# A two-layer decoder step on one core: second-layer units reordered, convolution chains one by one, output tiles scaled from PSUM

## The chip, the cores and the metric

One core of a Trainium2 chip runs the whole kernel as one launch. The metric is the device time in microseconds of that launch. Engines are named as in the profile: PE (TensorE matmul), PEld (its weight load), DVE (VectorE), ACT (ScalarE), POOL (GpSimd), SP (SyncE, which here only issues transfers).

## The reference, cut to what matters

Two layers, 2048 prompt rows and 64 sample rows of width 1024, float32. Both layers share a frame: pre-norm, one input projection to six groups of 512 channels, two mixers, one output projection, post-norm, residual.

```python
h = rms_norm(x, pre_g);  z = einsum("btd,de->bte", h, w_in)       # 1024 -> 6*512
# layer 0: a 3-tap gated convolution and a pooling mixer
# layer 1:
u, v, gc, za, zb, gd = split(z, 6)
yc = u * (tril(W_s) @ layer_norm(v) + b) * silu(gc)               # rows mixed in chunks of 128
yd = silu(layer_norm(dwconv31(za * sigmoid(zb)))) * silu(gd)      # 31 taps over the rows
o = einsum("bte,ed->btd", concat([yc, yd]), w_out)                # 1024 -> 1024
x = x + rms_norm(o, post_g)
```

The convolution of layer 1 has 31 taps for each of 512 channels, and its layer norm needs all 512 channels of a row, so a row of yd exists only when the convolution of all four channel blocks has passed it.

## The kernel before

**Stages.** The work is a list of 82 units in six stages: stages 0 and 1 are the input projection of layer 0 for the first and second 1024 rows, stage 2 its output projection, stages 3, 4 and 5 the same for layer 1. The sample rows ride along in stages 1 and 4. A unit of an input projection makes two blocks of 128 channels for 1024 rows with seven products of 12 matmuls (84), each matmul 128x512. Every operand is split into a high and a low part (`Bh`/`Bl` for activations, `ahi`/`alo` for weights), and each product takes three matmuls. A unit of an output projection ("z tile", `unit_z`) makes 128 rows by 1024 columns with 48 matmuls, into two PSUM banks: one tile uses `bank_a` and `bank_c`, the next the two `bank_b`. There are 17 z tiles in each layer, the 9th to 17th of layer 1 being the second 1024 rows and the sample.

**Units of layer 1** (`UNITS_O`): `d` makes a block's convolution input (za, zb), `v` the rows to be mixed, `u` the gate and product of the mixed rows, `g` the gate of the convolution. The `u` units need the mixing that follows the second `v`.

**The convolution** runs on DVE. `Dc.c21` puts each finished block's `chain(...)` into the list `chains`; `conv_proc`, the process of lowest priority, gives out one DVE instruction at a time. A chain splits even and odd rows: 31 taps into two sums `fa` and `fc` in turn (L1431 to L1442), then 16 taps with summed weights `wsum` into `fc` alone (L1454, L1458). Before, up to two chains take turns. After each 1024 rows and four blocks, `ln_tile` (L1829) reads 128 rows back, transposes them (PE, `yt`), normalises, transposes again (`yb`), multiplies with the gate (DVE, L1867) and stores to `yd`, from which a z tile loads its weights-side operand `araw` (split by ACT into `ahi` and by DVE, L452, into `alo`).

**The end of a z tile** (`post`, L1934): ACT copies each PSUM bank to an SBUF tile `o` as soon as it is full (L1054), which frees the bank; then ACT squares both (`junk`, L1946, a sum in `ss`), POOL makes the reciprocal root `rr` (three small instructions, L713 to L715), DVE scales both halves by `rr` and `gpost` (L1952), adds the residual `xres` (L1955), and POOL issues the stores. In layer 0 the tile is then normalised again (L1972), transposed (`tp`) and stored as input of layer 1.

**What sets the order.** The order on every engine is written out when the program is built: `Plan` keeps estimated clocks of the engines, processes say when they may go on, and `take_bank`, `U.take` and `a_need` let the plan's clock run on until a bank, a slot or a weight is there. On the chip each engine runs its list in order and waits on semaphores.

```python
yield ("c", lambda: len(chains) > 0 and (chains[0][1] is not None or U.room(3 if pl.relax else 6)))
turn = (turn + 1) % min(2, len(chains))
```

## Time and profile before

| | |
|---|---|
| median of 3 runs | 1587.73 us (1587.39 to 1588.47) |
| the profiled execution | 1585.21 us |
| its span, first to last instruction | 1583.5 us |
| PE busy | 1477.1 us, 93% of the span, 6746 instructions |
| DVE, ACT, POOL busy | 1089.1 (69%), 799.1 (50%), 460.8 us (29%) |
| moved by DMA | 408.14 MB, mean 258 GB/s |

The page's chain of work that ended last is almost all PE. A busy share is a mean over six stages and says little; the rows further down are cut by stage. The stages begin, by the count of the projection's matmuls (line L902; 1008 for an input stage, 816 for an output stage), at 0, 314.7, 582.6, 797.7, 1069.6 and 1357.2 us, and the last matmul ends at 1569.95 us.

### The profile page before, as it was taken

Reading aid. Unit: us, or ns where it says so; the run is one execution under the profiler, and the core shown is the slowest. Engines: PE = TensorE matmul, PEld = TensorE weight load, DVE = VectorE, ACT = ScalarE, POOL = GpSimd, SP = SyncE. Lnnn points to the kernel's source line nnn. Section 1 sums busy time; section 2 is a strip of 40 time slices with the busy share of each in tenths; the row PEclk is TensorE's granted clock in tenths of the full one; section 3 lists DMA queues with packets and bytes.
Section 4 is the critical chain, followed back from the end, with each engine's and each line's share of the span. In section 5 each row is a group of like instructions: output and inputs, shape, how many; then the busy total and the mean of one; then the engine's idle time right before and its main releaser. Section 6 shows DMA issues by size and latency. Waiting matters only on the chain. (4 is left out here: it accounts for less than half of the span.)

```text
span 1583.5 us, 22268 instructions
## 1 busy us (share of the span) xinstructions
PE 1477.1 (93%) x6746; PEld 1195.2 (75%) x6746; DVE 1089.1 (69%) x1843; ACT 799.1 (50%) x1680; POOL 460.8 (29%) x865
## 2 busy tenths in 40 slices
PE   4499998899999999999989999989999999999796
PEld 3277887788888887877767888867888887788675
DVE  4866788775656566577667678877865869894431
ACT  5455344664555465466564655455454464525521
POOL 4134333121121205575741421010122022324321
PEclk9699999999999999999999999999999999999898
DMA  7356879888897888799999889897557678738541
GB/s 279 128 189 221 291 268 325 277 276 303 287 323 273 309 262 270 245 317 310 348 361 353 304 311 323 278 330 238 183 187 237 206 245 298 241 129 246 152 149 42
DMA packets 232347, 408.14 MB, mean 258 GB/s; under 512 B 28705, under 2 KB 78129, under 8 KB 232226
## 3 DMA queue, kind: packets, MB, share of 16 engines
q1 hardware_dynamic: 192194, 277.23, 53.9%
q0 software_dynamic: 40032, 129.48, 21.9%
q8 instruction: 53, 0.87, 0.2%
q14 instruction: 68, 0.56, 0.1%
HBM read 277.16 MB, written 129.45 MB: 257 GB/s over the span
## 5 line engine op out<-in xcount | busy, mean ns | idle before, releaser
L902 PE MATMUL bank_b<-Bh,alo 128*128 128x512 f32 (+1 forms) x848 | 341.3, 402 | 4.0 <-DVE alo L452 3.9
L902 PE MATMUL bank_b<-Bl,ahi 128*128 128x512 f32 (+1 forms) x848 | 335.9, 396 | 4.0 <-ACT ahi L285 4.0
L902 PE MATMUL bank_b<-Bh,ahi 128*128 128x512 f32 (+1 forms) x848 | 335.0, 395 | 0.0
L285 ACT CAST ahi<-araw 128x512 fp32r<-128x512 f32 (+1 forms) x404 | 239.5, 618 | 14.8 <-issue 3.8
L902 PE MATMUL bank_c<-Bh,alo 128*128 128x512 f32 (+1 forms) x496 | 200.4, 404 | 10.0 <-ACT Bh L285 7.1
L902 PE MATMUL bank_a<-Bh,alo 128*128 128x512 f32 (+1 forms) x496 | 201.0, 405 | 6.6 <-DVE alo L452 5.1
L902 PE MATMUL bank_c<-Bl,ahi 128*128 128x512 f32 (+1 forms) x496 | 198.0, 399 | 9.5 <-ACT ahi L285 6.2
L902 PE MATMUL bank_a<-Bl,ahi 128*128 128x512 f32 (+1 forms) x496 | 198.4, 400 | 8.2 <-ACT ahi L285 7.1
L902 PE MATMUL bank_a<-Bh,ahi 128*128 128x512 f32 (+1 forms) x496 | 197.1, 397 | 0.0
L902 PE MATMUL bank_c<-Bh,ahi 128*128 128x512 f32 (+1 forms) x496 | 197.0, 397 | 0.0
L902 PEld LDWEIGHTS bank_b<-Bh,alo 128*128 128x128 f32 (+1 forms) x848 | 159.3, 188 | 41.5 <-DVE alo L452 3.4
L902 PEld LDWEIGHTS bank_b<-Bl,ahi 128*128 128x128 f32 (+1 forms) x848 | 159.6, 188 | 40.2 <-ACT ahi L285 4.9
L902 PEld LDWEIGHTS bank_b<-Bh,ahi 128*128 128x128 f32 (+1 forms) x848 | 159.3, 188 | 38.8
L452 DVE TENSOR_TENSOR alo<-araw,ahi 128x512 fp32r<-128x512 f32 (+1 forms) x164 | 108.6, 681 | 70.5 <-ACT ahi L285 61.6
L902 PEld LDWEIGHTS bank_c<-Bl,ahi 128*128 128x128 f32 (+1 forms) x496 | 93.9, 189 | 31.9 <-ACT ahi L285 7.7
L902 PEld LDWEIGHTS bank_c<-Bh,alo 128*128 128x128 f32 (+1 forms) x496 | 94.0, 189 | 31.0 <-ACT Bh L285 7.5
L902 PEld LDWEIGHTS bank_a<-Bl,ahi 128*128 128x128 f32 (+1 forms) x496 | 94.1, 190 | 30.2 <-ACT ahi L285 9.1
L902 PEld LDWEIGHTS bank_a<-Bh,alo 128*128 128x128 f32 (+1 forms) x496 | 94.0, 189 | 27.3 <-DVE alo L452 5.5
L902 PEld LDWEIGHTS bank_a<-Bh,ahi 128*128 128x128 f32 (+1 forms) x496 | 94.0, 190 | 22.5
L902 PEld LDWEIGHTS bank_c<-Bh,ahi 128*128 128x128 f32 (+1 forms) x496 | 93.9, 189 | 22.3
L1454 DVE SCALAR_TENSOR_TENSOR fc<-fs,wsum,fc 128x512 f32<-128x512 f32 x120 | 89.9, 749 | 2.9
L674 DVE TENSOR_TENSOR Bl<-braw,Bh 128x512 fp32r<-128x512 f32 x116 | 73.4, 686 | 24.7 <-ACT Bh L285 24.4
(269 smaller groups left out, 2464.7 us busy)
## 6 DMA issues: line engine op xcount, KB each, us to landing
araw<-wx SPq DMA_DIRECT2D x144, 256.0 KB
araw<-wsd SPq DMA_DIRECT2D x144, 256.0 KB
alo<-wld SPq DMA_DIRECT2D x144, 256.0 KB
alo<-wlx SPq DMA_DIRECT2D x96, 256.0 KB
praw<-wi SPq DMA_DIRECT2D x72, 256.0 KB
araw<-yd SPq DMA_DIRECT2D x64, 256.0 KB
araw<-wi SPq DMA_DIRECT2D x48, 256.0 KB
wld<-alo POOLq DMA_DIRECT2D x48, 256.0 KB, 3.9
```

The source lines that it names most:

```text
L285: nc.scalar.copy(out=out, in_=in_)
L452: nc.vector.tensor_tensor(out=lo, in0=x, in1=hi.bitcast(F32), op=SUB)
L674: nc.vector.tensor_tensor(out=Bl[j][:, k, :], in0=r, in1=Bh[j][:, k, :].bitcast(F32), op=SUB)
L902: nc.tensor.matmul(out=out[:m], lhsT=w[k][:, :m], rhs=r[:, k, :], start=(start and k == 0 and w is l), stop=(stop and k == KH - 1 and w is ...
L1454: nc.vector.scalar_tensor_tensor(out=C, in0=sm[:, j:j + HM], scalar=w, in1=C, op0=MUL, op1=ADD if j else SUB)
```

## The change

Three things. In layer 1 the two `v` units come first, and each `u` unit stands behind a `d` unit. The chains run one by one, in the order they are made, and a chain may begin with 5 free slots rather than 6. In `unit_z` the copies out of PSUM are gone: ACT squares straight from the bank, POOL's `rr` follows at once, and DVE's scale reads the bank, which is free only then. `post` waits for four slots rather than two and takes its `o` tiles itself; in layer 1 its DVE steps go half by half (scale, add, store, scale, add, store), and near the end (when the last unit is current) SP issues the stores in place of POOL.

```diff
-UNITS_O = [_d(0), ("v", 0, 4, 5), ("v", 1, 6, 7), _d(1), _u(0), _u(1), _d(2), _u(2), _d(3), _u(3),
+UNITS_O = [("v", 0, 4, 5), ("v", 1, 6, 7), _d(0), _u(0), _d(1), _u(1), _d(2), _u(2), _d(3), _u(3),
...
@@ unit_z
-            o.append(U.take([P, 512], "o"))
-            at = act(out=o[n][:m], in_=bk[:m])
-            done_bank(key)
+            banks.append((bk, key))
+            junk = sp.tile([P, 512], mybir.dt.bfloat16, tag="junk", name="junk", bufs=1)
+            at = act(out=junk[:m], in_=bk[:m], func=AF.Square, accum_out=ss[:m, n:n + 1])
+        r = rsq(ss, m)
...
@@ conv_proc
+            yield ("c", lambda: len(chains) > 0 and U.room(3 if pl.relax else 5))
+            for cost in chains[0]:
+                yield ("d", cost)
+            chains.pop(0)
...
@@ post
-        yield ("c", lambda: U.room(2))
+        yield ("c", lambda: U.room(4))
...
+        def scale(h):
             yield ("d", st_cost(512))
-            nc.vector.scalar_tensor_tensor(out=o[h][:n], in0=o[h][:n], scalar=r[:n], in1=gpost[h][:n], op0=MUL, op1=MUL)
+            bk, key = banks[h]
+            nc.vector.scalar_tensor_tensor(out=o[h][:n], in0=bk[:n], scalar=r[:n], in1=gpost[h][:n], op0=MUL, op1=MUL)
+            done_bank(key)
...
+            if lay and st["cur"] + 1 == len(seq):
+                nc.sync.dma_start(out=dst, in_=o[h][:n])
+                U.free()
+            else:
+                store(dst, o[h][:n], *((U.free,) if lay else ()))
+        for f, h in ((scale, 0), (add, 0), (scale, 1), (add, 1)) if lay else ((scale, 0), (scale, 1), (add, 0), (add, 1)):
```

The order that the plan makes of it, at three places.

**Place 1: DVE, the end of the last convolution chain** (second 1024 rows, fourth block), in stage 5. L1458 is the chain's last step; the scale rows are z tiles. Before:

```order
L1454 SCALAR_TENSOR_TENSOR fc<-fs,wsum,fc 128x512 x5
L1952 SCALAR_TENSOR_TENSOR o<-o,rr,gpost 128x512 x2
L1955 TENSOR_TENSOR o<-o,xres 128x512 x2
L452 TENSOR_TENSOR alo<-araw,ahi 128x512
L1454 SCALAR_TENSOR_TENSOR fc<-fs,wsum,fc 128x512 x10
L1952 SCALAR_TENSOR_TENSOR o<-o,rr,gpost 128x512 x2
L1955 TENSOR_TENSOR o<-o,xres 128x512 x2
L1458 SCALAR_TENSOR_TENSOR glu<-fs,wsum,fc 128x256 x2
```

After (L1939 is the scale, L1944 the add):

```order
L1939 SCALAR_TENSOR_TENSOR o<-bank_b_104,rr,gpost 128x512
L1454 SCALAR_TENSOR_TENSOR fc<-fs,wsum,fc 128x512
L1944 TENSOR_TENSOR o<-o,xres 128x512
L1939 SCALAR_TENSOR_TENSOR o<-bank_b_105,rr,gpost 128x512
L1944 TENSOR_TENSOR o<-o,xres 128x512
L1454 SCALAR_TENSOR_TENSOR fc<-fs,wsum,fc 128x512 x2
L452 TENSOR_TENSOR alo<-araw,ahi 128x512
L1454 SCALAR_TENSOR_TENSOR fc<-fs,wsum,fc 128x512 x2
L1458 SCALAR_TENSOR_TENSOR glu<-fs,wsum,fc 128x256 x2
```

Before, the chain's end stands behind the scales of the fifth z tile of the stage; now behind those of the third. The fifth of the second half's nine gate products (L1867, now L1855), which the tenth z tile needs, stood behind the scales of the ninth tile and now stands behind those of the seventh.

**Place 2: DVE, from the last z tile of stage 2 into stage 3.** `bank_b_104` and `_105` hold the 16th tile, `bank_a` and `bank_c` the 17th; the first matmul of stage 3 writes `bank_a`. Before:

```order
L1952 SCALAR_TENSOR_TENSOR o<-o,rr,gpost 128x512
L1955 TENSOR_TENSOR o<-o,xres 128x512 x2
L674 TENSOR_TENSOR Bl_89<-braw,Bh_82 128x512 x3
L1930 TENSOR_TENSOR xres<-xres 128x512 x2
L1972 SCALAR_TENSOR_TENSOR xres<-o,rr,gpre_5443 128x512
L1972 SCALAR_TENSOR_TENSOR xres<-o,rr,gpre_5445 128x512
L1930 TENSOR_TENSOR xres<-xres 128x512 x2
L1952 SCALAR_TENSOR_TENSOR o<-o,rr,gpost 128x512 x2
```

After:

```order
L1939 SCALAR_TENSOR_TENSOR o<-bank_b_105,rr,gpost 128x512
L674 TENSOR_TENSOR Bl_86<-braw,Bh_79 128x512
L1944 TENSOR_TENSOR o<-o,xres 128x512
L674 TENSOR_TENSOR Bl_86<-braw,Bh_79 128x512
L1944 TENSOR_TENSOR o<-o,xres 128x512
L674 TENSOR_TENSOR Bl_86<-braw,Bh_79 128x512 x2
L645 TENSOR_TENSOR praw<-praw 128x512
L1939 SCALAR_TENSOR_TENSOR o<-bank_a,rr,gpost 128x512
L674 TENSOR_TENSOR Bl_89<-braw,Bh_82 128x512 x4
L1969 SCALAR_TENSOR_TENSOR xres<-o,rr,gpre_5443 128x512
L630 TENSOR_TENSOR plo<-praw,plo 128x512
L1969 SCALAR_TENSOR_TENSOR xres<-o,rr,gpre_5445 128x512
```

The 17th tile's first scale moved ahead of the second normalisation (L1969, was L1972) and of L1918 (was L1930), and the scale of `bank_c` follows the last row shown.

**Place 3: the last stores.** POOL's last rows before:

```order
L262 DMA o_xp<-o 128x512 x2
L713 TENSOR_TENSOR ss<-ss 128x1
L714 TENSOR_SCALAR ss<-ss 128x1
L715 TENSOR_TENSOR rr<-ss,half 128x1
L262 DMA o_xp<-o 128x512 x2
```

SP's last rows after, where before there were only the loads of `xres`:

```order
L1928 DMA xres<-x1d 64x512 x2
L1928 DMA xres<-x1d 128x512 x2
L1953 DMA o_xp<-o 128x512 x2
L1928 DMA xres<-x1d 128x512 x2
L1953 DMA o_xp<-o 128x512 x2
```

The stores of the last two z tiles moved from POOL to SP; POOL now ends with `rr`, and the last tile's `xres` loads stand behind the stores of the tile before it.

## Rows read from the trace of the kernel before

**Rows 1.** Stretch: length; busy (instructions) of PE, PEld, DVE, ACT, POOL; PEclk; DMA share; GB/s.

```profile
797.70:867.80 70.10, 60.41 (x251) 47.05 (x251) 50.49 (x85) 37.44 (x76) 23.42 (x34) 0.95 1.00 362
...
1084.00:1327.00 243.00, 242.83 (x1226) 202.49 (x1225) 180.45 (x319) 123.17 (x254) 42.35 (x74) 1.00 0.67 215
...
1380.46:1391.62 11.16, 11.16 (x49) 9.00 (x49) 9.96 (x16) 3.56 (x8) 3.31 (x5) 1.00 0.49 153
1449.45:1462.69 13.24, 12.75 (x61) 10.24 (x61) 6.14 (x12) 8.00 (x18) 7.02 (x13) 1.00 1.10 324
1462.69:1491.07 28.38, 19.30 (x83) 15.40 (x82) 14.16 (x24) 15.97 (x34) 10.85 (x21) 0.82 0.55 159
...
sum 1583.50, PE 1477.12 PEld 1195.17 DVE 1089.05 ACT 799.11 POOL 460.80; mean PE 123.09 PEld 99.60 DVE 90.75 ACT 66.59 POOL 38.40
```

**Rows 2.** PE in time: start, us, and in brackets idle before and what ended it.

```profile
1478.88 0.79 PE L902 MATMUL bank_a<-Bh,alo 128*128 128x512 f32 x1 [5.07 <-DVE alo L452]
```

**Rows 3.** DVE in time (start, us): last chain's begin and end, fifth gate product.

```profile
1341.82 0.70 DVE L1426 TENSOR_TENSOR fs<-glu 128x527 f32<-128x527 f32 x1
...
1421.64 0.88 DVE L1458 SCALAR_TENSOR_TENSOR glu<-fs,wsum,fc 128x256 f32<-128x256 f32 x2
...
1470.33 0.69 DVE L1867 TENSOR_TENSOR lny<-lny,lng 128x512 f32<-128x512 f32 x1 [0.40 <-ACT lny L287]
```

**Rows 4.** DVE in time: taps in turn, and ten taps into one sum.

```profile
1389.23 0.75 DVE L1442 SCALAR_TENSOR_TENSOR fc<-glu,cst,fc 128x512 f32<-128x512 f32 x1
1389.90 0.75 DVE L1433 SCALAR_TENSOR_TENSOR fa<-glu,cst,fa 128x513 f32<-128x513 f32 x1
...
1411.35 7.84 DVE L1454 SCALAR_TENSOR_TENSOR fc<-fs,wsum,fc 128x512 f32<-128x512 f32 x10
```

**Rows 5.** Groups by line and form: busy us, mean ns of one, idle before.

```profile
L285 ACT COPY o<-bank_b 128x512 f32<-128x512 f32 x32 | 18.7, 585 | 66.6 <-PE bank_b L902 64.7 <-issue 1.8
L287 ACT ACTIVATE ga<-bank_b 128x512 f32<-128x512 f32 x8 | 4.8, 595 | 7.6 <-PE bank_b L902 7.5
...
L1952 DVE SCALAR_TENSOR_TENSOR o<-o,rr,gpost 128x512 f32<-128x512 f32 x64 | 45.7, 753 | 34.6 <-POOL rr L715 34.6
L1131 DVE SCALAR_TENSOR_TENSOR win<-pm,cst,sgb 128x512 f32<-128x512 f32 x16 | 12.0, 750 | 14.3 <-PE pm L1127 13.4 <-PE pm L1125 1.0
```

**Rows 6.** In time: end of the tenth and 17th tile of stage 2, their scales.

```profile
710.41 0.57 ACT L285 COPY o<-bank_b 128x512 f32<-128x512 f32 x1
...
724.23 1.41 DVE L1952 SCALAR_TENSOR_TENSOR o<-o,rr,gpost 128x512 f32<-128x512 f32 x2
...
797.51 0.39 PE L902 MATMUL bank_c<-Bh,ahi 128*128 128x512 f32 x1
...
817.93 1.41 DVE L1952 SCALAR_TENSOR_TENSOR o<-o,rr,gpost 128x512 f32<-128x512 f32 x2
```

**Rows 7.** Waits of PE from 780 to 870.

```profile
PE bank_c L902 <- ACT ahi L285: 4.7, 3, 2.8
PE bank_c L902 <- ACT bank_b L285: 2.9, 1, 2.9
PE bank_a L902 <- ACT ahi L285: 2.1, 3, 1.0
```

**Rows 8.** Waits of PE from 582 to 798.

```profile
PE tp L1982 <- DVE xres L1972: 4.2, 3, 1.6
```

**Rows 9.** The end, in time: after the last matmul.

```profile
1571.22 0.63 ACT L287 ACTIVATE junk<-o 128x512 bf16<-128x512 f32 x1
...
1572.03 0.19 POOL L713 TENSOR_TENSOR ss<-ss 128x1 f32<-128x1 f32 x1 [6.48 <-ACT junk L287]
...
1573.18 1.42 DVE L1952 SCALAR_TENSOR_TENSOR o<-o,rr,gpost 128x512 f32<-128x512 f32 x2 [8.52 <-POOL rr L715]
...
1575.49 1.15 POOL L262 DMA_DIRECT2D o_xp<-o  x2 [2.35 <-DVE o L1955]
```

**Rows 10.** Transfers issued on POOL for the result: KB each, median us to landing.

```profile
o_xp<-o POOLq DMA_DIRECT2D x32, 256.0 KB, 3.0
```

More of the change, by code (lines that the diff above doesn't have):

```diff
@@ L1038, in unit_z @@
         m, t0 = (NSAMP, NPR) if i < 0 else (P, i * P)
-        o = []
+        banks, ss = [], sp.tile([P, 2], F32, tag="ss", name="ss", bufs=4)
         for n in range(2):
@@ L1052, in unit_z @@
                     a_done(u, h)
-            o.append(U.take([P, 512], "o"))
-            at = act(out=o[n][:m], in_=bk[:m])
-            done_bank(key)
+            banks.append((bk, key))
+            junk = sp.tile([P, 512], mybir.dt.bfloat16, tag="junk", name="junk", bufs=1)
+            at = act(out=junk[:m], in_=bk[:m], func=AF.Square, accum_out=ss[:m, n:n + 1])
+        r = rsq(ss, m)
         def go():
-            yield ("u", at)
-            yield from post(lay, t0, m, o, (i // 8 * 4 + i % 4, i % 8 // 4))
+            yield from post(lay, t0, m, banks, r, at + 2.2, (i // 8 * 4 + i % 4, i % 8 // 4))
         pl.spawn(go(), 2)
@@ L1485, in conv_proc @@
     def conv_proc():
-        turn = 0
         while True:
-            yield ("c", lambda: len(chains) > 0 and (chains[0][1] is not None or U.room(3 if pl.relax else 6)))
-            turn = (turn + 1) % min(2, len(chains))
-            if chains[turn][1] is None and not U.room(9):
-                turn = 0
-            c = chains[turn]
-            if c[1] is None:
-                if not U.room(3):
-                    continue
-                c[1] = next(c[0])
-                continue
-            yield ("d", c[1] + (0.12 if len(chains) == 1 else 0.0))
-            try:
-                c[1] = next(c[0])
-            except StopIteration:
-                chains.remove(c)
-                if st.get("conv_end") and not chains:
-                    return
+            yield ("c", lambda: len(chains) > 0 and U.room(3 if pl.relax else 5))
+            for cost in chains[0]:
+                yield ("d", cost)
+            chains.pop(0)
+            if st.get("conv_end") and not chains:
+                return
     class Dc:
@@ L1562, in proc @@
                     act(out=old[:, e, :], in_=g[e][:, HM:HM + HE], dep=pl.dve + 0.12)
-                chains.append([chain(self.s, self.cb, g[0], g[1]), None])
+                chains.append(chain(self.s, self.cb, g[0], g[1]))
             pl.spawn(proc(), 1)
@@ L1575, in smp @@
             aux_free()
-            chains.append([chain_s(cb, t), None])
+            chains.append(chain_s(cb, t))
     vs = {}
@@ L1932, in h_t, with post @@
                   lambda j=j: put(j, 0), U.free)
-    def post(lay, t0, n, o, ie=None):
-        xr = []
-        yield ("c", lambda: U.room(2))
+    def post(lay, t0, n, banks, r, at, ie=None):
+        xr, o = [], []
+        yield ("c", lambda: U.room(4))
         for h in range(2):
@@ L1942, in post, with add @@
             xr.append(t)
-        ss = sp.tile([P, 2], F32, tag="ss", name="ss", bufs=4)
-        junk = sp.tile([P, 512], mybir.dt.bfloat16, tag="junk", name="junk", bufs=1)
         for h in range(2):
-            at = act(out=junk[:n], in_=o[h][:n], func=AF.Square, accum_out=ss[:n, h:h + 1])
-        r = rsq(ss, n)
-        yield ("u", max(at + 2.2, xat))
+            o.append(U.take([P, 512], "o"))
         gpost, gpre = rows["gpost"], rows.get("gpre")
-        for h in range(2):
+        yield ("u", at)
+        def scale(h):
             yield ("d", st_cost(512))
-            nc.vector.scalar_tensor_tensor(out=o[h][:n], in0=o[h][:n], scalar=r[:n], in1=gpost[h][:n], op0=MUL, op1=MUL)
-        for h in range(2):
+            bk, key = banks[h]
+            nc.vector.scalar_tensor_tensor(out=o[h][:n], in0=bk[:n], scalar=r[:n], in1=gpost[h][:n], op0=MUL, op1=MUL)
+            done_bank(key)
+        def add(h):
             yield ("d", tt_cost(512))
@@ L1962, in post @@
                 dst = a["o_xp"][t0:t0 + n, c]
-            store(dst, o[h][:n], *((U.free,) if lay else ()))
+            if lay and st["cur"] + 1 == len(seq):
[4 more added lines that the diff above has]
+        for f, h in ((scale, 0), (add, 0), (scale, 1), (add, 1)) if lay else ((scale, 0), (scale, 1), (add, 0), (add, 1)):
+            if h == 0 and f is add:
+                yield ("u", xat)
+            yield from f(h)
         if lay == 1:
```

## The prediction, made blind

> **What bounds the kernel now.** I read the busy table by stretch first, then the waits of PE, then time lines of the places found. PE is busy 1477 of 1583.5 us [rows 1], so only some 106 us can be won without taking matmuls away, and the change takes none away. I therefore look for where PE stands still, and ask which of those places the change touches.
>
> The largest place behind the start is in stage 5. [...] The tile waits for its operand: its second half starts again at 1478.88, after 5.07 us of waiting for DVE's `alo` [rows 2]. That operand comes out of the fifth gate product of the second half, at 1470.33, and this out of the last convolution chain, which ends at 1422.5 (1421.64 + 0.88) [rows 3]. So the end of that chain sets 13 us of the program. The second place is the step from stage 2 to 3: 9.7 us idle of 70.1 (70.10 - 60.41) with the DMA engines at a share of 1.00 [rows 1]; 2.9 us of it waits for a PSUM bank and 6.8 for weight halves [rows 7]. The third is the end, 13.55 us after the last matmul at 1569.95.
>
> **The last chain ends earlier.** At place 1 of the order its last step moves from behind the fifth z tile's scales to behind the third's. The third tile is the undisturbed one, which ends at 1391.62 [rows 1]. Behind that come the square and `rr` (2.0 us, worked out at the end below), two scales and adds, five taps at 0.78 (7.84 for ten [rows 4]), a split and the last step; with what stands between, 10 us. The chain then ends near 1402, some 20 us earlier. From the chain's end to the fifth product 47.8 us passed (1470.33 - 1422.5), from there to the restart 8.6 (1478.88 - 1470.33) [rows 2, 3]: 1458, while the tile cannot begin before 1462.69 [rows 1]. The wait goes, with 4 us to spare; next late would be nothing that I can find in stage 5.
>
> What it is worth: the tenth tile holds 83 - 48 = 35 transposes, which must still be done. The ninth holds 13 in 13.24 us, 0.49 of them idle: (12.75 - 11.16) / 13 = 0.12 us each, so 4.3 us for 35. 28.38 - 11.16 - 4.3 = **12.9 us gained**. Bounds: nothing at all, and 12.9.
>
> **What the earlier end costs.** The first `d` unit comes two units later in each half, the second one later. That costs nothing while DVE has idle time to catch up: from 1084 to 1327 it is busy 180 of 243 us [rows 1]. One chain alone also makes each tap of its second part wait for the one before: 0.78 us apart instead of 0.67 for two sums in turn (1389.90 - 1389.23) [rows 4]. At most 15 taps in 8 chains, 13 us of DVE work, hidden by the same 63 idle us; 1.7 us in the last chain, inside the 4 to spare. The `u` units find their mixed rows as before, since one unit still lies between the second `v` and the first `u`.
>
> **No copies, scale from PSUM.** ACT loses 68 copies of 0.585 us [rows 5], 40 us, but it is busy half the time and this is on the path only at the end. A square read from a bank should cost what the gate read from a bank costs, 0.595 us, and DVE's scale reads a bank at the price of SBUF: 750 ns for the same form out of PSUM (L1131), 753 out of SBUF [rows 5].
> [...]
>
> The price is that a bank is held. Before, a copy freed it 0.6 us after its last matmul; now it waits for square, `rr` and DVE's turn. Inside a stage a bank is wanted again 11 to 12 us after its tile's end. In stage 5 DVE now does the scale 5 to 6 us after, so nothing waits. In stage 2 DVE is late at times: the tenth tile's scales ended 14.9 us (first of them, 724.98) after its last matmul near 710.1 [rows 6], which in the new kernel would be 2.7 us of waiting; but the scale now stands right behind the tile in DVE's order. I take 0, with bounds of -4.2 (the waits for `tp` gone [rows 8]) and +5 (two such tiles).
>
> At place 2 the wait is certain. Stage 3 begins with `bank_a`, and before its scale DVE has nine instructions of about 0.65 us in its order from the first scale of the 16th tile on: 9 x 0.65 + 0.75 = 6.6 us after the last matmul, if DVE comes to them on time; `rr` is ready by then. `bank_c` follows seven instructions later, at 11.9, and is wanted at 6.6 + 2.8 = 9.4: 2.5 more. Together 9.1. Against it stand the 9.7 us that PE idles there now; the loads go on during the new wait, so I let the waits for weight halves vanish in it: **0.6 gained**. Bounds: 5 gained, if DVE is ahead and only `rr` counts (2.0 + 0.75, then 2.5), and 14 lost, if the scale comes as late as it does today, 20 us after the last matmul (817.93 - 797.9 [rows 6]).
> [...]
>
> **The end.** Only the last half-tile's square is left behind the last matmul: from the square's start to POOL 0.81 us (1572.03 - 1571.22), POOL 1.15 (1573.18 - 1572.03) [rows 9]; so `rr` at 1569.95 + 2.0. Scale, add, scale, add take 2.9, and the last store is issued at 1574.85 rather than 1576.07: 1.2 us. Today 7.4 us pass from that issue to the end of the span, of which the landing takes 3.0 [rows 10]; the other 4.4 show no work. If they hang on POOL, which now ends with `rr`, up to 4.2 us go (1576.07 - 1571.9). I take **3.5**, near the upper bound because no row shows anything else to wait for; bounds 1.2 and 4.2.
>
> **Sum.** 12.9 + 0.6 + 3.5 = 17.0 us. The profiled execution took 1585.2 us, 2.5 under the median of the runs; against it 1568.2, against the median **1570.7 us**.
>
> **Rivals.**
> 1. *The normalisation, not the convolution, holds the tenth tile.* Its transposes now stand in PE's order between z matmuls, and POOL and ACT have to turn them round. For: only 4 us to spare. Against: the fifth product moved two tiles forward. Half of the 12.9 stays: 1577; all of it: 1583.6. Chance 0.10.
> 2. *Banks.* The scales come as late as today: 14 + 5 lost, 16.4 gained: 1590, no measurable change. For: DVE waits in order for transfers before them in stage 2. Against: the new order puts the scales ahead of those. Chance 0.08.
> 3. *The convolution does not catch up: slower.* Place: DVE in stage 4. If the 21.8 us by which the second `d` unit comes later (a unit with sample rows) carry through to the last chain's end, the tenth tile waits 21.8 longer instead of 12.9 less: +21.8 - 4.1, 1605. It decides from 7 us later than 1422.5 on. Against: DVE idles 63 us in that stretch. Chance 0.07.
> 4. *More goes.* The waits for weight halves and for `tp` vanish, the end gives 4.2: 12.9 + 5 + 4.2 + 4.2 = 26, 1561. Chance 0.13.
>
> **How the numbers follow.** The forecast has 0.62, alone 1564 to 1577. The range 1561 to 1584 takes in rivals 1 and 4 and leaves out 0.15. A measurement of this kernel can tell about 0.2% (3 us) from no change. Faster by more: forecast, rivals 1 and 4, 0.85. Within: rival 2, 0.08. Slower: rival 3, 0.07.
>
> **What would show it.** Right: the last L1458 in stage 5 near 1390 to 1405, the tenth z tile at 12 to 13 us with a granted clock of 1.00; 6 to 7 us of PE waiting for DVE before the first matmul of stage 3, and the loss of the stretch around it near today's 9.7; no wait of PE for a scale in stage 5; under 11 us from the last matmul to the end. Wrong: a wait for `alo` still standing in the tenth tile (rival 1), waits of PE for L1939 in stage 2 or over 12 us at stage 3 (rival 2), the last chain's end after 1425 (rival 3).

## The result, and the profile after

The changed kernel takes **1562.31 us** (median of 4 runs, 1559.45 to 1566.23) against 1587.56 us before in the same comparison (4 runs, 1586.87 to 1588.47): a ratio of **0.9842, 95% interval 0.9820 to 0.9864**, so 25.2 us faster where 17.0 were forecast. Its profiled execution took 1559.45 us with a span of 1557.7, 25.8 less than the span before. The measured time lies below the forecast's own band (1564 to 1577) and 1.3 us inside the range (1561 to 1584). One of the six executions of last_copied, a run further down, took 3432.05 us; what is said of that run goes by the other five.

The stages are cut in both traces at the first L902 matmul of each. Stages 0 and 1 took 557.1 us before and 556.6 after. The rest:

| | before | after | difference | forecast |
|---|---|---|---|---|
| stages 2 and 3 | 486.9 | 478.9 | -8.0 | -0.6 |
| stage 4 | 287.7 | 288.5 | +0.9 | 0 |
| stage 5 | 212.8 | 199.5 | -13.3 | -12.9 |
| last matmul to the end of the span | 13.6 | 8.3 | -5.3 | -3.5 |

Now the views. The busy table by stretch, columns as in [rows 1]: stage 3's first 70 us, and the ninth and tenth z tile of stage 5.

```profile
797.50:867.50 70.00, 68.99 (x315) 56.08 (x316) 30.36 (x55) 40.61 (x84) 25.11 (x48) 0.96 0.99 369
...
1445.48:1458.09 12.61, 12.61 (x63) 10.33 (x62) 7.54 (x13) 7.49 (x18) 6.24 (x12) 1.00 0.72 209
1458.09:1470.94 12.85, 12.63 (x62) 10.09 (x60) 8.26 (x14) 6.17 (x14) 6.29 (x13) 1.00 0.87 250
```

PE idles 1.0 us of the 70 where it idled 9.7, with the DMA engines as full as before (0.99, before 1.00). The stretch begins behind a wait of PE of 3.9 us, which is counted in stage 2. The tenth tile, whose wait for its operand the prediction starts from, takes 12.85 us at a granted clock of 1.00, before 28.38 at 0.82 [rows 1]. DVE in time: the last convolution chain's begin and end and the fifth gate product of the second half, which answer to [rows 3]:

```profile
1318.16 0.70 DVE L1426 TENSOR_TENSOR fs<-glu 128x527 f32<-128x527 f32 x1
...
1395.00 0.88 DVE L1458 SCALAR_TENSOR_TENSOR glu<-fs,wsum,fc 128x256 f32<-128x256 f32 x2
...
1443.36 0.69 DVE L1855 TENSOR_TENSOR lny<-lny,lng 128x512 f32<-128x512 f32 x1 [3.35 <-ACT lny L287]
```

The chain ends at 1395.9 (1395.00 + 0.88), before at 1422.5; the product comes 14.7 us ahead of the tenth tile (1458.09 - 1443.36), where it came 7.6 us after that tile had begun [rows 1, 3]. The waits of PE from 780 to 870, in place of [rows 7]:

```profile
PE bank_a L902 <- DVE o L1939: 3.9, 1, 3.9
PE bank_c L902 <- DVE o L1939: 1.0, 1, 1.0
```

In this stretch all waits for weight halves (`ahi`) are gone; two waits for scales have come. The groups by line and form, for [rows 5], show what the two operations that now read PSUM cost:

```profile
L1939 DVE SCALAR_TENSOR_TENSOR o<-bank_b,rr,gpost 128x512 f32<-128x512 f32 x32 | 23.3, 745 | 14.8 <-POOL rr L715 14.8
...
L287 ACT ACTIVATE junk<-bank_b 128x512 bf16<-128x512 f32 x32 | 19.1, 596 | 71.7 <-PE bank_b L902 61.8 <-issue 9.8
```

And the end in time, for [rows 9]; the last matmul ends at 1549.46:

```profile
1549.06 0.40 PE L902 MATMUL bank_b<-Bh,ahi 128*128 128x512 f32 x1
1549.55 0.60 ACT L287 ACTIVATE junk<-bank_b 128x512 bf16<-128x512 f32 x1 [4.92 <-issue]
...
1550.31 0.19 POOL L713 TENSOR_TENSOR ss<-ss 128x1 f32<-128x1 f32 x1 [10.08 <-ACT junk L287]
...
1551.45 0.75 DVE L1939 SCALAR_TENSOR_TENSOR o<-bank_b,rr,gpost 128x512 f32<-128x512 f32 x1 [8.31 <-POOL rr L715]
...
1552.95 1.73 SPq L1953 DMA_DIRECT2D o_xp<-o  x2
```

Both stores are issued by 1554.68; the span ends 3.0 us later. Before, 6.9 us passed between (1575.49 + 1.15 to 1583.5) [rows 9].

### The profile page after: what moved, and what is told of

It reads as the page before. It is cut to its first block, busy times and chain, and to the rows that moved or that the text cites. A ratio compares the mean times of both kernels' runs of the same rounds, so it can differ in the third digit from the quotient of the medians.

```text
span 1557.7 us, 22197 instructions
## 1 busy us (share of the span) xinstructions
PE 1471.7 (94%) x6746; PEld 1193.6 (77%) x6746; DVE 1090.8 (70%) x1843; ACT 769.3 (49%) x1616; POOL 446.3 (29%) x861
## 4 chain that ended last, share of the span: by engine, by line
PE 75%; issue 10%; DMA 5%; DVE 4%; POOL 3%; ACT 2%; SPq 0%; POOLq 0%; DVEq 0%; ACTq 0%
PE bank_b L902 31%; PE bank_c L902 18%; PE bank_a L902 18%; PE bank L902 1%; PE zs L913 1%; PE zs L914 1%; DVE Bl L674 1%; PE sg L1596 1%; PE tp L1979 1%; DMA sgd<-sgd 1%; DVE xT L796 1%; DMA wsd<-asum 1%; DVE xT L743 1%; PE zf L930 1%; ACT xrow L287 1%
## 5 line engine op out<-in xcount | busy, mean ns | idle before, releaser
L902 PE MATMUL bank_b<-Bh,alo 128*128 128x512 f32 (+1 forms) x848 | 340.2, 401 | 4.0 <-DVE alo L452 4.0
L902 PE MATMUL bank_b<-Bl,ahi 128*128 128x512 f32 (+1 forms) x848 | 335.7, 396 | 4.0 <-ACT ahi L285 4.0
L902 PE MATMUL bank_b<-Bh,ahi 128*128 128x512 f32 (+1 forms) x848 | 335.0, 395 | 0.0
L902 PE MATMUL bank_a<-Bh,alo 128*128 128x512 f32 (+1 forms) x496 | 202.2, 408 | 7.5 <-DVE o L1939 3.9
L902 PE MATMUL bank_c<-Bh,alo 128*128 128x512 f32 (+1 forms) x496 | 199.5, 402 | 8.0 <-ACT Bh L285 7.0
L902 PE MATMUL bank_a<-Bl,ahi 128*128 128x512 f32 (+1 forms) x496 | 198.2, 400 | 6.4 <-ACT ahi L285 5.3
L902 PE MATMUL bank_c<-Bl,ahi 128*128 128x512 f32 (+1 forms) x496 | 197.0, 397 | 5.1 <-DVE Bl L674 3.4
L902 PE MATMUL bank_a<-Bh,ahi 128*128 128x512 f32 (+1 forms) x496 | 197.2, 398 | 0.0
L902 PE MATMUL bank_c<-Bh,ahi 128*128 128x512 f32 (+1 forms) x496 | 196.2, 396 | 0.0
L902 PEld LDWEIGHTS bank_b<-Bh,alo 128*128 128x128 f32 (+1 forms) x848 | 159.1, 188 | 40.9 <-DVE alo L452 2.6
L902 PEld LDWEIGHTS bank_b<-Bl,ahi 128*128 128x128 f32 (+1 forms) x848 | 159.4, 188 | 40.4 <-ACT ahi L285 4.9
L902 PEld LDWEIGHTS bank_b<-Bh,ahi 128*128 128x128 f32 (+1 forms) x848 | 159.2, 188 | 38.5
L902 PEld LDWEIGHTS bank_c<-Bh,alo 128*128 128x128 f32 (+1 forms) x496 | 93.4, 188 | 29.5 <-ACT Bh L285 7.5
L902 PEld LDWEIGHTS bank_a<-Bh,alo 128*128 128x128 f32 (+1 forms) x496 | 94.0, 189 | 28.2 <-DVE o L1939 4.4
L902 PEld LDWEIGHTS bank_a<-Bl,ahi 128*128 128x128 f32 (+1 forms) x496 | 94.1, 190 | 27.2 <-ACT ahi L285 6.6
L902 PEld LDWEIGHTS bank_c<-Bl,ahi 128*128 128x128 f32 (+1 forms) x496 | 93.4, 188 | 27.4 <-DVE Bl L674 5.1
L902 PEld LDWEIGHTS bank_a<-Bh,ahi 128*128 128x128 f32 (+1 forms) x496 | 94.0, 190 | 22.7
L902 PEld LDWEIGHTS bank_c<-Bh,ahi 128*128 128x128 f32 (+1 forms) x496 | 93.4, 188 | 22.5
```

What stands on the lines that cost most here:

```text
L902: nc.tensor.matmul(out=out[:m], lhsT=w[k][:, :m], rhs=r[:, k, :], start=(start and k == 0 and w is l), stop=(stop and k == KH - 1 and w is ...
```

## The experiments

Three readings were to be separated: which part brings stage 5's 13 us, which brings the 8 us of stages 2 and 3, which the 5 us at the end. All twelve runs in one table; a time, where the edit starts from, and four lengths in us from each trace. "Chain end" is the end of the last L1458, counted from the first matmul of stage 5; "tile 10" goes from the tenth z tile's first matmul to the eleventh's (28.7 before by this cut).

| run | starts from | median | ratio to before, 95% interval | stages 2+3 | chain end | tile 10 | stage 5 | end |
|---|---|---|---|---|---|---|---|---|
| before | | 1587.6 | | 486.9 | +65.3 | 28.7 | 212.8 | 13.6 |
| after | | 1562.3 | 0.9842 (0.9820 to 0.9864) | 478.9 | +45.9 | 12.8 | 199.5 | 8.3 |
| f_order | before | 1602.0 | 1.0084 (1.0060 to 1.0108) | 489.8 | +88.2 | 27.6 | 229.5 | 12.9 |
| f_chain | before | 1570.3 | 0.9877 (0.9855 to 0.9899) | 486.8 | +9.1 | 11.2 | 198.0 | 13.3 |
| f_psum | before | 1576.4 | 0.9916 (0.9893 to 0.9940) | 480.9 | +66.1 | 26.7 | 209.8 | 11.5 |
| f_all_pool | after | 1566.8 | 0.9858 (0.9832 to 0.9884) | 476.5 | +45.9 | 13.0 | 199.6 | 11.3 |
| old_order | after | 1562.4 | 0.9849 (0.9823 to 0.9876) | 480.1 | -3.7 | 11.2 | 197.6 | 8.4 |
| b_room5 | before | 1574.4 | 0.9921 (0.9897 to 0.9945) | 484.3 | +14.6 | 11.1 | 200.4 | 13.6 |
| b_one6 | before | 1574.8 | 0.9916 (0.9895 to 0.9938) | 486.6 | +21.4 | 11.2 | 198.9 | 13.3 |
| room6 | after | 1593.5 | 1.0041 (1.0025 to 1.0058) | 478.7 | +89.9 | 27.3 | 230.1 | 8.6 |
| after_turns5 | after | 1565.9 | 0.9868 (0.9850 to 0.9886) | 479.9 | +61.9 | 19.3 | 207.5 | 8.3 |
| psum_copy | f_psum | 1592.4 | 1.0033 (1.0016 to 1.0050) | 491.2 | +69.6 | 27.0 | 213.1 | 9.8 |
| last_copied | after | 1568.5 | 0.9883 (0.9863 to 0.9903) | 483.2 | +45.7 | 12.8 | 201.1 | 8.0 |
| only_last | f_psum | 1591.2 | 1.0025 (1.0012 to 1.0038) | 490.7 | +66.1 | 26.8 | 211.3 | 12.7 |

Stage 0, which no edit touches, takes 288.7 to 293.1 us in these traces, and stages 2 and 3 of after and f_all_pool, where the programs are alike, differ by 2.4; a difference of 2 to 4 us in one trace proves little without its waits.

### Each part alone

**f_order**: the unit order alone.

```diff
-UNITS_O = [_d(0), ("v", 0, 4, 5), ("v", 1, 6, 7), _d(1), _u(0), _u(1), _d(2), _u(2), _d(3), _u(3),
+UNITS_O = [("v", 0, 4, 5), ("v", 1, 6, 7), _d(0), _u(0), _d(1), _u(1), _d(2), _u(2), _d(3), _u(3),
```

> Only the order of the second layer's units is changed (both v units first, each u behind a d); the chains still take turns and the output tiles are still copied out of PSUM. Theory (the 13 us of stage 5 come from the last chain's earlier end, which the one-by-one rule brings): in this kernel's order the last chain's end stands behind 12 scales of stage 5, before behind 10, after behind 6; so it ends about 11 us later than 1422.5, near 1433, the tenth z tile waits about as much longer (28 us becomes 35 to 40) and stage 5 grows by 7 to 12 us. Rival (the unit order frees DVE early and that gives the 13 us): the tenth tile shrinks to 13 us, stage 5 gives 13. On stage 3 the theory that the order brings its 7.8 us (v units load less work on DVE and ACT at the start) expects 264 us there instead of 272; the rival that the missing copies bring them expects 272. Sum: 1580 to 1597 by the theory, about 1567 by the rival.

Measured 1602.0 us, 14.5 over before and beyond the theory's range: the order alone makes the kernel slower. The chain ends 23 us later against the stage's start, more than the 11 expected, and stage 5 grows by 16.8. The place differs from what was expected: the tenth tile is not longer, the second (20.6 us) and the ninth (19.8) are. PE in time, in these three tiles:

```profile
1384.53 0.80 PE L902 MATMUL bank_a<-Bh,alo 128*128 128x512 f32 x1 [5.72 <-DVE alo L452]
...
1471.97 1.12 PE L1859 MATMUL yb<-ident,yv 128*128 128x128 f32 x4 [2.99 <-ACT yv L287]
...
1491.95 1.11 PE L1859 MATMUL yb<-ident,yv 128*128 128x128 f32 x4 [3.18 <-ACT yv L287]
...
1501.34 0.80 PE L902 MATMUL bank_a<-Bh,alo 128*128 128x512 f32 x1 [6.58 <-DVE alo L452]
```

The operands of z tiles are late in both halves. So the theory had the direction right, and the size and the tile wrong. Stage 3 gives nothing: 272.4 us, before 271.8. Its first four units take 100.1 us and the next six 120.3, where before they took 95.6 and 125.8; the mixing's matmuls have moved between them.

**f_chain**: the chains alone, one by one and begun with five free slots.

```diff
...
+            yield ("c", lambda: len(chains) > 0 and U.room(3 if pl.relax else 5))
+            for cost in chains[0]:
+                yield ("d", cost)
+            chains.pop(0)
...
```

> Only the chains are changed: one by one, begun with five free slots rather than six; unit order and copies out of PSUM as before. Theory: the last chain's end stands ahead of every scale of stage 5 (before behind 10), so it ends near 1365, the tenth z tile takes 12 to 13 us with the granted clock at 1.00, stage 5 falls from 212.8 to about 199.5: 1585 - 13 = 1572 to 1575. The rival by unit order expects the tenth tile unchanged, 1585 to 1588. Stage 3: 272 by both theories on it (neither the order nor the copies are touched), 264 only if the one-by-one chains are what relieves its start. End: 13.5 us from the last matmul, as before.

Measured 1570.3, 17.2 under before and 2 under the range; stage 5 at 198.0, nothing in stage 3 (273.4) or at the end. The tenth tile, columns as in [rows 1]:

```profile
1468.82:1479.98 11.16, 11.16 (x49) 9.00 (x48) 4.01 (x6) 3.56 (x8) 2.09 (x5) 1.00 0.48 152
```

It is as short as the undisturbed tile of [rows 1]. The chain part brings stage 5's gain by itself.

**f_psum**: squares and scales from PSUM, with all stores on POOL.

```diff
-            o.append(U.take([P, 512], "o"))
-            at = act(out=o[n][:m], in_=bk[:m])
-            done_bank(key)
+            banks.append((bk, key))
...
+            at = act(out=junk[:m], in_=bk[:m], func=AF.Square, accum_out=ss[:m, n:n + 1])
...
```

This part also moves the plan's wait for the residual's load (`xat`) from ahead of the scale to ahead of the add, which lets DVE's list have the scale earlier; no run takes that apart from the missing copies.

> Only the output tiles are changed: squared and scaled from PSUM, half by half in the second layer, with all stores still issued by POOL; unit order and chains as before. Theory: the last chain still stands behind 10 scales of stage 5, so the tenth tile stays at 28 us and stage 5 at 212.8. Stage 3: about 264 us if the missing copies and their slots are what let the weight halves come in time, 272 plus the wait for bank_a if not (272 to 277). End: 12.3 us from the last matmul (13.55 less 1.2) if the stores on SP make the rest, 8 to 9 us if the half-by-half steps make it all. Sum: 1577 to 1582.

Measured 1576.4, 11.1 under before. Stages 2 and 3 are 6.0 us shorter, the first four units of stage 3 alone 10.7 (95.6 to 84.9), the end 2.0 (between the two theories' numbers); the tenth tile stays at 26.7. PE in time at stage 3's start, its only waits there:

```profile
804.54 0.79 PE L902 MATMUL bank_a<-Bh,alo 128*128 128x512 f32 x1 [3.94 <-DVE o L1951]
...
810.62 0.50 PE L902 MATMUL bank_c<-Bh,alo 128*128 128x512 f32 x1 [0.60 <-DVE o L1951]
```

The gain in stages 2 and 3 comes with this part: 6.0 us alone, 8.0 in the changed kernel. By stage, f_chain's 14.7 (stage 5) and f_psum's 6.0 and 2.0, with 3.0 for SP below, make 25.7, about the whole difference of the two spans. That the sum comes so close is partly chance: in the changed kernel stage 5 gives 13.3, and the medians of the parts don't add up (17.2 and 11.1 under before, f_order 14.5 over).

**f_all_pool**: the changed kernel with its last stores on POOL.

```diff
-            if lay and st["cur"] + 1 == len(seq):
-                nc.sync.dma_start(out=dst, in_=o[h][:n])
-                U.free()
-            else:
-                store(dst, o[h][:n], *((U.free,) if lay else ()))
+            store(dst, o[h][:n], *((U.free,) if lay else ()))
```

> The changed kernel with the last stores issued by POOL again; all else as after. Theory (the stores on SP give some 4 of the 5.3 us at the end, since the program closes sooner behind a transfer of SP than behind one of POOL): 12 to 12.5 us from the last matmul to the end instead of 8.24, the time 3.5 to 4.5 us over the changed kernel's, near 1563.5 to 1566.5. Rival (squaring the last half alone and going half by half shorten the end): 8 to 9 us, no difference in time. Stages 2 to 5 as in the changed kernel by both.

The end takes 11.3 us, neither the 12 to 12.5 of the theory nor the rival's 8 to 9. So SP's stores bring 3.0 of the 5.3 (11.3 - 8.3), and the rest, 2.3, comes without SP. The medians differ by 4.5 us in the same sense, but the two intervals overlap. The last two issues in time; the span ends at 1561.7:

```profile
1554.14 0.61 POOL L262 DMA_DIRECT2D o_xp<-o  x1 [1.81 <-DVE o L1944]
...
1555.53 0.54 POOL L262 DMA_DIRECT2D o_xp<-o  x1 [0.78 <-DVE o L1944]
```

From the end of the last issue to the end of the span pass 5.6 us (1561.7 - 1556.07), with SP 3.0. What POOL does there is a closing DRAIN, an instruction at the end of its list that the view by source line shows; each row gives shortest, median and longest duration in ns, and first and last start. The long one is the first. Before, f_all_pool, after:

```profile
L2196 POOLq DRAIN  x3: 40/102/6366, 1576.1 to 1583.2; - x3
L2189 POOLq DRAIN  x3: 40/93/5384, 1555.5 to 1561.4; - x3
L2193 POOLq DRAIN  x3: 40/93/5096, 1550.8 to 1557.5; - x3
```

With the stores on POOL, the DRAIN begins at the last issue and ends about 1 us before the span does (1576.1 + 6.4 of 1583.5, 1555.5 + 5.4 of 1561.7). With the stores on SP it begins at POOL's last `rr` and is over 1.8 us before the end (1550.8 + 5.1 of 1557.7): it has run beside the last scales and stores. So SP's 3.0 us come from that overlap.

### Which condition lets the last chain end early

**old_order**: the changed kernel with the unit order of before.

```diff
-UNITS_O = [("v", 0, 4, 5), ("v", 1, 6, 7), _d(0), _u(0), _d(1), _u(1), _d(2), _u(2), _d(3), _u(3),
+UNITS_O = [_d(0), ("v", 0, 4, 5), ("v", 1, 6, 7), _d(1), _u(0), _u(1), _d(2), _u(2), _d(3), _u(3),
```

> The changed kernel with the unit order of before put back; one-by-one chains, scaling from PSUM and the last stores on SP stay. Theory (the order of the units gives nothing and costs 5 us early in stage 3, 24.9, 19.6, 23.9, 22.2 for its first four units where the kernel with scaling from PSUM alone took 24.6, 19.5, 19.5, 21.3; the other two parts give all): the last chain ends ahead of every scale of stage 5, stage 5 takes 198 to 199.5 us, stage 3 259 to 264, the end 8.3, and the time is 0 to 6 us under the changed kernel's 1562, near 1558. Rival (the parts need one another, the order keeps the chains' slots free once the output tiles hold them longer): stage 5 returns to 205 or more and the time to 1568 or more.

Measured 1562.4: the same time as the changed kernel, where some 4 us less was expected. The chain ends 50 us earlier against stage 5's start and that brings 1.9 us; it had been early enough. The 5 us that the order seemed to cost in stage 3's first units come back in the next six, as in f_order. So the new order neither brings nor costs anything that these runs can tell, once the other two parts are there.

**b_room5** and **b_one6**: the two conditions of the chain part, each alone, on the kernel before.

```diff
-yield ("c", lambda: len(chains) > 0 and (chains[0][1] is not None or U.room(3 if pl.relax else 6)))
+yield ("c", lambda: len(chains) > 0 and (chains[0][1] is not None or U.room(3 if pl.relax else 5)))
```

> The kernel before with one number changed: a chain may begin with five free slots rather than six; the chains still take turns. Theory (it is when the last chain may begin, not the turns, that set its end): it begins 168 projection matmuls ahead of stage 5 rather than 37 and ends behind 61 of them rather than 281, so the tenth z tile takes 11 to 13 us, stage 5 198 to 200 and the time is near 1572, as with the one-by-one chains. Rival (taking turns stretches each chain, and only one-by-one shortens it): the tenth tile keeps 20 us or more, 1580 or more.

```diff
-            yield ("c", lambda: len(chains) > 0 and U.room(3 if pl.relax else 5))
+            yield ("c", lambda: len(chains) > 0 and U.room(3 if pl.relax else 6))
```

This second diff starts from f_chain.

> The kernel before with the chains one by one, but a chain begins, as before, with six free slots. Theory (what counts is where the last chain's end stands in DVE's list, by whatever means it got there): it stands behind 92 projection matmuls of stage 5 and 2 scales (before 281 and 10), so the end comes near 1380, the tenth tile takes 11 to 13 us, stage 5 198 to 201, the time 1570 to 1576, as with either of the other two ways. Rival (the number five is needed, as in the changed kernel, where six cost 31 us of stage 5): the tenth tile keeps 20 us or more, 1580 or more.

Measured 1574.4 and 1574.8, tile 10 at 11.1 and 11.2 us, stage 5 at 200.4 (0.4 over its range) and 198.9: on the old order either condition is enough for the tenth tile. Both medians are 4 us over f_chain's, which the tenth tile does not explain.

**room6**: the changed kernel with six slots. The diff is that of b_one6.

> The changed kernel with one number put back: a chain begins with six free slots rather than five. Theory (the number is what lets the last chain begin): the chain begins behind 132 projection matmuls of stage 5 instead of 86 ahead of it, and ends behind 372 instead of 192, later than before (281); the tenth tile waits 27 us or more, stage 5 takes 213 to 235 us, and the time is 1575 to 1598. Rival (one-by-one alone gives the early end whatever the number): stage 5 at 199.5, 1562.

Measured 1593.5, slower than before; the chain ends 44 us later than in the changed kernel (+89.9 against +45.9) and stage 5 grows by 30.6. Here the ninth tile takes 32.5 us as well, by a wait of the same kind:

```profile
1465.47 0.80 PE L902 MATMUL bank_b<-Bh,alo 128*128 128x512 f32 x1 [6.76 <-DVE alo L452]
```

With the new order one-by-one needs the five.

**after_turns5**: the changed kernel with chains in turn, begun with five slots.

```diff
...
-            for cost in chains[0]:
-                yield ("d", cost)
-            chains.pop(0)
...
+            turn = (turn + 1) % min(2, len(chains))
...
+            yield ("d", c[1] + (0.12 if len(chains) == 1 else 0.0))
...
```

> The changed kernel with the chains taking turns again, two at a time, but begun with five free slots as in the changed kernel. In DVE's list the last chain's end then stands behind 254 projection matmuls of stage 5 and 8 scales (changed kernel 192 and 6, before 281 and 10). Theory (the place of that end in the list decides, and the tenth tile begins to wait once the end comes some 4 us later than 8 us behind the changed kernel's 1396): the end comes near 1407 to 1410, the tenth tile takes 13 to 20 us, stage 5 200 to 208, the time 1562 to 1571. Rival (five slots alone give all, as they did on the kernel before): the tenth tile at 12.8, stage 5 at 199.5, the time 1559 to 1565. Other rival (one-by-one is needed with the new order): the tenth tile at 25 or more, stage 5 at 212 or more, 1574 or more.

Measured 1565.9, chain end at 1410.3, tile 10 at 19.3, stage 5 at 207.5: the chain's end at the upper edge of the theory's numbers, the rest within them. Tile and stage lie outside both rivals' numbers; the time, 0.9 over the first rival's, does not tell the two apart. The tenth tile, and what PE waits for in it:

```profile
1457.66:1476.97 19.31, 15.26 (x70) 12.12 (x68) 11.20 (x19) 9.93 (x23) 8.82 (x15) 0.91 0.81 222
```

```profile
1464.97 0.66 PE L1859 MATMUL yb<-ident,yv 128*128 128x128 f32 x4 [3.48 <-ACT yv L287]
...
1466.20 0.80 PE L902 MATMUL bank_a<-Bh,alo 128*128 128x512 f32 x1 [0.58 <-DVE alo L452]
```

The waits make 4.1 us. Behind them the first matmul takes 0.80 us and the next six 0.63 each, where those at the tile's start take 0.39; the granted clock over the tile is 0.91. Read down the table, chain end against tile 10: up to +21.4 the tile takes 11.1 or 11.2 us, at +45.7 to +45.9 12.8 to 13.0, at +61.9 19.3, at +65.3 and later 26.7 to 28.7. Which edit brought the chain there makes no difference to the tenth tile. The step lies between +46 and +62. Where the chain ends later still (f_order, room6), the tenth tile grows no further; the ninth does (19.8 and 32.5 us).

### Where the waits for weight halves went

**psum_copy**: f_psum with a copy of each bank into the scratch tile `junk` ahead of the square; nothing reads it.

```diff
+            act(out=junk[:m], in_=bk[:m])
             at = act(out=junk[:m], in_=bk[:m], func=AF.Square, accum_out=ss[:m, n:n + 1])
```

> Scaling from PSUM alone, as in the earlier run, plus a copy of each bank into the scratch tile junk, read by nobody, ahead of each square: ACT's 68 copies of 0.585 us are back, but no slot is taken by them. Theory (what held the weight halves at stage 3's start was that a copy waited for a free slot, with the casts of the weights behind it on ACT): the first four units of stage 3 stay at 85 us and stage 3 at 262 to 264, since ACT waits for no slot; the time is within 3 us of 1576. Rival (ACT's time and place in its list): the four units return to 90 to 95 us, stage 3 to 270 or more, the time to 1583 or more.

Measured 1592.4, 16 over f_psum: the theory's time fails. Time and the first four units (92.7 us) are the rival's numbers, stage 3 (268.1) lies between the two. But the waits are not those of before. PE from 780 to 900:

```profile
PE bank_c L902 <- DVE o L1952: 4.6, 1, 4.6
PE bank_a L902 <- DVE o L1952: 4.0, 1, 4.0
PE bank_c L902 <- ACT ahi L285: 1.0, 1, 1.0
```

Weight halves stay nearly punctual although ACT has its copies back. That does not clear ACT's time, since PE waits 8.6 us for banks ahead of them, in which ACT can catch up. Stages 2 and 3 are 5 us longer each than in f_psum; 4.1 of these are longer waits for banks (8.6 against 4.5 us). The rest of the 16 was not traced.

**last_copied**: the changed kernel, with ACT's copy back for the last tile of stage 2 alone.

```diff
+        copied = lay == 0 and u + 1 == phase_units[ph][1]
...
+            if copied:
+                t = U.take([P, 512], "o")
+                act(out=t[:m], in_=bk[:m])
+                done_bank(key)
+                bk, key = t, None
             banks.append((bk, key))
...
```

> The changed kernel, but the last output tile of stage 2, and it alone, is copied out of PSUM again by ACT before it is squared and scaled. It asks where the weight halves' waits of stage 3 went (9.7 us of PE idle in its first four units before, 1.0 after, with 3.9 us of waiting for bank_a ahead of them). Theory (head start: PE's new wait for bank_a is what lets the weight halves get ahead, ACT casting them while PE stands): bank_a is free 0.6 us after its last matmul, the 3.9 and 1.0 us go, and the waits for ahi come back, 4 to 8 us in the first four units: no gain, 1560 to 1566. Rival (the missing copies and their slots relieve ACT's list, and the wait for bank_a is pure loss): neither wait is there, stages 2 and 3 together lose 4 to 5 us, the time is near 1557 and the best of all.

Measured 1568.5, 6.2 over the changed kernel and 2.5 beyond the head start's range; stages 2 and 3 make 4.3 of it. The waits for the banks are gone and those for weight halves are back: PE idles 8.0 us of the first four units (after: 1.0), 7.0 of it for `ahi`. PE in time:

```profile
804.80 0.80 PE L902 MATMUL bank_c<-Bl,ahi 128*128 128x512 f32 x1 [3.81 <-ACT ahi L285]
811.06 0.50 PE L902 MATMUL bank_b<-Bl,ahi 128*128 128x512 f32 x1 [0.77 <-ACT ahi L285]
819.25 0.50 PE L902 MATMUL bank_b<-Bl,ahi 128*128 128x512 f32 x1 [1.48 <-ACT ahi L285]
832.51 0.50 PE L902 MATMUL bank_c<-Bl,ahi 128*128 128x512 f32 x1 [0.97 <-ACT ahi L285]
```

**only_last**: the opposite. f_psum with copies for all tiles but the last of stage 2.

```diff
+        copied = not (lay == 0 and u + 1 == phase_units[ph][1])
...
```

> The kernel with scaling from PSUM alone, but only the last output tile of stage 2 is scaled from PSUM; all other output tiles are copied out first (and squared right behind the copy). Theory (head start): with PE waiting for bank_a before stage 3 as there, 2 to 8 us, the waits for ahi in the first four units fall from 9.7 us before to 0 to 3. Rival (it is the copies of all the tiles, in ACT's list and in the slots, that make the weight halves late): the waits for ahi stay at 6 to 10 us and the wait for bank_a stands on top of them. Stage 5 and its tenth tile as before by both (212 us; the last chain stands behind 10 scales), the time 1578 to 1595.

Measured 1591.2. PE waits once, for 14.1 us rather than 2 to 8, and in the four units behind that it idles 0.6 us; they take 84.0 us. PE, and below it DVE, in time:

```profile
814.41 0.80 PE L902 MATMUL bank_a<-Bh,alo 128*128 128x512 f32 x1 [14.09 <-DVE o L1957]
```

```profile
810.95 1.42 DVE L1936 TENSOR_TENSOR xres<-xres 128x512 f32<-128x512 f32 x2 [4.50 <-DMA td<-xres]
812.29 1.41 DVE L1984 SCALAR_TENSOR_TENSOR xres<-o,rr,gpre 128x512 f32<-128x512 f32 x2
813.61 0.74 DVE L1957 SCALAR_TENSOR_TENSOR o<-bank_a,rr,gpost 128x512 f32<-128x512 f32 x1
```

By the waits for `ahi` the head start holds in both directions. In all fourteen traces: wherever PE waits for `bank_a` ahead of stage 3 (after, f_psum, f_all_pool, old_order, room6, after_turns5, psum_copy, only_last), the waits for weight halves in the first four units come to 1.0 us or nothing. Wherever it doesn't (before, f_order, f_chain, b_room5, b_one6, last_copied), PE idles 8 to 10 us there, spread over the units.

The traces also show who gets ahead. Before, ACT is busy for 8.28 of the 8.31 us between the last matmul of stage 2 (it ends at 797.90 [rows 6]) and the cast of `ahi` that PE waits for. ACT, then PE:

```profile
806.21 1.12 ACT L285 CAST ahi<-araw 128x512 fp32r<-128x512 f32 x2
```

```profile
806.86 0.80 PE L902 MATMUL bank_c<-Bl,ahi 128*128 128x512 f32 x1 [2.81 <-ACT ahi L285]
```

After, the last matmul of stage 2 ends at 793.57 (793.18 + 0.39), and ACT's next cast of `ahi` begins 5.0 us later. PE, then ACT:

```profile
793.18 0.39 PE L902 MATMUL bank_c<-Bh,ahi 128*128 128x512 f32 x1
```

```profile
798.58 0.62 ACT L285 CAST ahi<-araw 128x512 fp32r<-128x512 f32 x1
```

ACT is busy throughout here too (4.92 of 5.01 us), with 12 instructions in that stretch where it had 21 before. So ACT's list made this half late, and two things help: ACT comes to the cast 3.3 us earlier, and PE comes to its matmul 4.9 us later. An estimate of their shares: without a wait for a bank, PE wants the half 3.0 us behind the last matmul (in last_copied at 804.80 - 3.81 = 800.99, with the last matmul ending at 797.96). After, the cast ends 5.6 us behind it. The shorter list alone would leave a wait of 2.6 us, and PE's wait covers that. The five casts that follow are early too: in f_psum, with the unit order of before, they begin 2.8 to 5.6 us earlier against the last matmul. Together with PE's own lateness that is more than any later wait of before (at most 1.0 us each), so a wait of 4 us can save 7 to 9. Neither share was tried by itself; that would take two runs with one order on ACT and PE's wait in only one of them.

## Why the prediction was right, point by point

**The last chain ends earlier: right in place, mechanism and size.** Forecast was the chain's end near 1402 with stage 5 beginning at 1357.2, that is +44.8; measured +45.9 (1395.9 in absolute time, since stage 5 began 7 us earlier). The tenth tile at 12 to 13 us and full clock: 12.85 and 1.00. Gained in stage 5: 13.3 against 12.9. From the chain's end to the fifth product pass 47.5 us (1443.36 - 1395.88), forecast 47.8. The tile itself gave 15.9, and the others took 2.6 back, as their transposes moved forward; with the 1.7 by which the tenth stands above 11.16 that makes the 4.3 us forecast for the transposes. The new wait looked for in its place (rival 1) was not there. after_turns5 and room6 show how near it stood: a chain end 16 us later brings back 6.5 of the tile's 15.9 us, one 44 us later makes stage 5 longer than before.

**Which edit does it** the prediction did not separate. It is the chain part; the unit order by itself moves the chain's end the wrong way, by 23 us.

**What the earlier end costs: nothing visible, as forecast.** DVE is busy for 199.7 of the 242 us from 1078 to 1320, more than before (180.5 of 243 [rows 1]), and the chain is on time all the same. Rival 3, the convolution that doesn't catch up, did not occur in this kernel. f_order, at 1602, is near the 1605 that it was given, and its chain ends 23 us later where the rival had 21.8; but there the second and ninth tile grow and not the tenth.

**Scale from PSUM costs what it costs from SBUF: right.** 745 ns from `bank_b`, 753 before from SBUF; the square from the bank 596, forecast 595 [rows 5]. By bank, the 64 scales of 128x512 take 744 to 747 ns.

**From stage 2 to stage 3: right in sign, one term mis-sized.** Forecast were 6.6 us of waiting for `bank_a` and 2.5 for `bank_c`, 9.1 in all; the waits are 3.9 and 1.0, 4.9 in all. The step that failed is the start of the sum: "DVE has nine instructions of about 0.65 us in its order from the first scale of the 16th tile on", counted from the last matmul. DVE in time:

```profile
791.06 1.40 DVE L1939 SCALAR_TENSOR_TENSOR o<-bank_b,rr,gpost 128x512 f32<-128x512 f32 x2
...
796.70 0.74 DVE L1939 SCALAR_TENSOR_TENSOR o<-bank_a,rr,gpost 128x512 f32<-128x512 f32 x1
```

The nine instructions are there and take 5.64 us without a pause (796.70 - 791.06), 0.63 each. But the first of them begins 2.5 us ahead of the last matmul's end (793.57) and not at it, so the bank is free 3.9 us behind that end. POOL's `rr` comes at 796.59 (795.71 + 0.88), so an earlier DVE would have won next to nothing more:

```profile
795.71 0.88 POOL L715 TENSOR_TENSOR rr<-ss,half 128x1 f32<-128x1 f32 x1
```

The other bound, "if DVE is ahead and only `rr` counts", has nearly the same sum (2.75 and 2.5, 5.25), but by luck: its first part is 1.2 too short and its second 1.5 too long.

Against 9.7 us of idle before, 4.7 are gained. The weight halves' waits did vanish, as the prediction let them; last_copied and only_last show that they go when PE waits. But its ground, "the loads go on during the new wait", names only part: the first late half hung on ACT's casts, not on a load. The 2.9 us that the prediction read as waiting for a bank [rows 7] were probably a load. In f_chain, whose order is the same at this place, the matmul in question begins before the copy that [rows 7] names has ended (805.76 against 805.98), and the profile puts its wait to the load of a low weight half. PE, then ACT:

```profile
805.76 0.47 PE L902 MATMUL bank_c<-Bh,alo 128*128 128x512 f32 x1 [2.28 <-DMA alo<-wld]
```

```profile
805.40 0.58 ACT L285 COPY bank_b<-bank_a 128x512 f32<-128x512 f32 x1
```

Of the other 3.3 us in stages 2 and 3, the wait for `tp` gives 1.9 (2.3 left of 4.2 [rows 8]), inside the bounds given for stage 2; the rest is within what two traces of one program differ by. Rival 2, the banks, is what only_last shows: DVE stuck behind a transfer, 14.1 us lost at that place, no gain in the whole. At this place a copy made at once is not the cheaper way: last_copied makes it for one tile and is 6.2 us slower than the changed kernel, in which PE waits 4.9 us for the held banks; in only_last holding the bank costs 14.1 us.

**The end: right in sign, outside its bounds.** Forecast 3.5 with bounds 1.2 and 4.2, measured 5.3; "under 11 us" was right at 8.3. What failed was the upper bound of 4.2, which let POOL's last work come earlier and kept all that follows it as long as before. Its condition, that the last 4.4 us "hang on POOL", holds: before, POOL's closing DRAIN ends 12.5 us behind the last matmul (1576.1 + 6.4 - 1569.95). After, it begins 4.8 us earlier against the last matmul, is 1.3 us shorter and ends at 6.4, 1.8 us ahead of the span's end. SP's part of the 5.3 is 3.0. Of the other 2.3, which f_all_pool keeps, 1.0 is the earlier last issue (forecast 1.2) and 1.0 the shorter DRAIN (5.4 against 6.4), which nothing forecast.

In sum, 17.0 was 8 short: some 4 from the bank waits, 2 from `tp`, 2 from the end. That is rival 4, "more goes", worked out there as 26 us and 1561, and given 0.13: the forecast's mechanisms are the right ones, but the number that came is the rival's.

No run beats the changed kernel; old_order ties with it.

## What to carry to other kernels

When a wait of PE is put in a step in which another engine is behind, count what gets ahead during it: here ACT was busy without a pause, and 4.9 us of waiting replaced 9.7. When operations are listed in a fixed order, the place of the last link of a long chain in that list, against its consumer, is the number to work out; how it gets there (fewer slots demanded, no turns) is secondary, and beyond the point of need an earlier end is worth next to nothing (here 50 us earlier brought 1.9). Parts of a change should be priced alone: one part here loses 14.5 us by itself and nothing in company.
